# A decoder layer on eight cores: instruction order from per-stage streams and a rough clock, or from one dependency graph and a list scheduler over all engines

## The chip, the cores and the metric

The kernel runs on the 8 cores of one Trainium2 chip. Each core does the whole layer for 2 of the 16 sequences; nothing passes between cores. The metric is the device time of the slowest core, in microseconds (us).

A core has several engines that each run their own instruction list in order: PE (matrix products), DVE (vector), ACT (activation functions), POOL (a second, slower vector engine: an f32 sum of 128x512 took 1.41 us on it and 0.71 us on DVE in the profile before), SP (only starts transfers here). They wait for each other by semaphores. The order in which instructions are put in these lists is fixed when the kernel is built. A badly placed instruction stalls everything behind it in its list (in the profile before, PE once stood for 7.03 us ahead of work that did not need the wait), and this case is about that order.

The program has two states. In some executions the four cores of one die are granted a lower PE clock than the other four, and the time is longer (in the first run of the changed kernel 0.81 to 0.82 against 0.98 to 0.99 of full speed, and up to 3064 us against 2646); such a run is called slow.

## The reference

The layer is a half-weighted SwiGLU FFN, a mixer with two kinds of attention, and a second half-weighted FFN, each between two RMS norms. The sizes are 2048 tokens a sequence, width 1024, FFN width 2816.

```python
x = x + 1/2 * post1(SwiGLU_1(pre1(x)))
x = x +       post2(W_out [DiffAttn(groupA) ; DilatedAttn(groupB)])   # both from ONE projection of pre2(x)
x = x + 1/2 * post3(SwiGLU_2(pre3(x)))

def swiglu(x, w_gate, w_up, w_down):
    return (jax.nn.silu(x @ w_gate) * (x @ w_up)) @ w_down
# DiffAttn: 4 heads, causal, a = softmax(q1 k1) - lam * softmax(q2 k2), values of width 128, then a per-head RMS norm
# DilatedAttn: 8 heads of width 64, patterns (window, dilation) = (128,1), (512,4), (2048,16), mixed by their denominators
# both with ALiBi: score += -slope * distance
```

Both kernels work on 8 "units" of attention a sequence: units 0 to 3 are one differential head each (below: diff), units 4 to 7 are two dilated heads each (below: dilated). A unit is cut into steps. A step multiplies a block of keys with 512 queries on PE (these products are called scores), takes the exponential on ACT, masks or weights on DVE, and multiplies with the values on PE. A diff unit has 40 steps and a dilated one 18.

## The kernel before

Both kernels do the FFN products with 7 block products in place of 8, which needs sums and differences of weight blocks (DVE) and of activations. Half a sequence is done at a time. The order of work in the kernel before is sequence 0: FFN1, attention, FFN2; then the same for sequence 1. The sums are made for the first sequence and stored, and loaded for the second. Part of this preparation runs inside attention:

```python
def weight_sums(F, bF, SB, bS, eng, cost):          # four DVE operations a pair of weight blocks
    for j, a, b, op, rd in ((0, F(2), F(3), ALU.add, [bF[1]]), (1, SB(0), F(0), ALU.subtract, [bS[0], bF[0]]),
                            (2, F(1), SB(1), ALU.subtract, [bF[0], bS[1]]), (3, F(0), F(2), ALU.subtract, bF)):
        ...
def push_prep(s):                                   # a stream of jobs beside attention
    ...
    for j in range(len(jobs)):
        ...  # load(j + 1) on POOL's queue, the four sums on DVE, then store(j) on SP's
```

The order of instructions comes from a rough clock. `_advance` adds an assumed cost to the time of an engine, and side work waits in streams of items. An item is put in when the clock says that it would be ready within a slack:

```python
def can_run(it, force=False):
    ...
    t = S.t[PE]
    if it.eng != PE and S.t[it.eng] > t + SLACK[it.eng]:
        return False
    ...
    return S.ready(rd, wr, it.eng) <= t + SLACK[it.eng]

# main loop of attention: what does PE do next: scores, fill (projections), values
t = S.t[PE]
...
if r_s <= first + EPS_T:
    pick = "S"
elif r_f <= first + EPS_T and (fill.urgent or behind or forced or r_a > first + EPS_T):
    pick = "F"
elif r_a <= first + EPS_T:
    pick = "A"
else:
    pick = "F"
```

For the head with the steepest slope the exponential of a step is split into four, each with its own bias.

The softmax here doesn't subtract the row's maximum and nothing guards it: scores larger than these inputs give would overflow.

## Time and profile before

The first three runs took 3361.25, 3153.83 and 3228.06 us (median 3228.06). The profiled run is a fast one.

The head of the page of the profiled run: the span, the busy time of each engine, the busy tenths of PE and its granted clock in 40 equal slices, and the chain of work that ended last, by engine.

```profile
span 3091.0 us, 51661 instructions; the slowest of 8 cores (3068.5 to 3091.0 us)
...
PE 2603.4 (84%) x16608; PEld 1346.4 (44%) x16608; DVE 1671.9 (54%) x2740; ACT 1431.6 (46%) x2186; POOL 616.5 (20%) x636
...
PE   3998998667788867987999999877888887799996
...
PEclk9999999779899988998999999988899999899998
...
PE 65%; DMA 11%; DVE 10%; ACT 6%; issue 6%; SPq 1%; POOL 0%; DVEq 0%; ACTq 0%; POOLq 0%
```

PE is busy for 84%, but the chain is only 65% PE: a fifth of it is transfers and DVE. The two valleys in the row of PE (slices 8 to 15 and 27 to 34) are the two attentions, and the clock dips in the same slices. Cut by stage, as busy times in stretches (columns: stretch and length, then busy us and instruction count of PE, its weight loads, DVE, ACT and POOL, then granted clock, DMA share, GB/s): the two attentions are lines one and four; lines two and three are a gate/up half of the FFN with sums remade, and one with sums loaded.

```profile
510.40:1146.50 636.10, 470.12 (x4233) 274.89 (x4232) 354.00 (x694) 339.77 (x523) 88.55 (x133) 0.89 0.54 121
1394.50:1550.10 155.60, 141.13 (x619) 61.56 (x620) 109.41 (x143) 61.08 (x82) 61.95 (x54) 0.95 0.58 128
1830.70:1966.80 136.10, 133.77 (x619) 60.20 (x618) 79.19 (x101) 62.37 (x85) 49.92 (x38) 1.00 0.69 210
2058.90:2631.20 572.30, 460.04 (x4231) 269.93 (x4231) 310.63 (x609) 330.48 (x508) 58.21 (x92) 0.92 0.33 79
```

In attention no engine is near full: PE is busy 470 of 636 us and 460 of 572 us, so 278 us of PE idle in the two, and DVE and ACT 53 to 58%. A gate/up half that remakes its sums took about 20 us longer than one that loads them, at a clock of 0.95 against 1.00. The waits of PE in the first attention (columns: engine, line, releaser: us in all, times, longest us; in the tile names, ps is the kernel's tensor in PSUM, to which PE writes its products, and M the one in SBUF, from which PE reads its operands):

```profile
PE ps L739 <- DVE M L732: 20.9, 2, 10.5
PE ps L1569 <- DVE M L1586: 16.3, 14, 2.3
PE ps L1272 <- DVE M L1241: 15.6, 6, 10.8
PE ps L1371 <- ACT M L1393: 14.2, 16, 2.7
```

There is no single large wait. There are many releasers, and the longest waits are 7 to 11 us, far longer than the operations waited for (those in these lines take 0.4 to 1.3 us in the mean). The timeline of PE shows one (start us, busy us, operation; in brackets the idle time before and its releaser). PE stands for 7 us before four transposes, although projections, which don't need them, follow in its list:

```profile
652.29 0.63 PE L1410 MATMUL ps<-M 128*128 128x129 bf16 x8
659.95 0.58 PE L1471 MATMUL ps<-ident,M 128*128 128x128 f16 x4 [7.03 <-DVE M L1282]
```

In the FFN, PE waits for weight sums, and DVE waits until the store of older sums has read its buffer. From the waits of the whole run:

```profile
PE ps L1013 <- DVE M L887: 46.2, 14, 14.3
...
DVE M L887 <- DMA sgu<-M: 47.5, 14, 11.0
```

Two groups of DVE instructions: the post-norm multiply and the normalisation of the dilated heads (count, then busy us and mean ns, then idle time before).

```profile
L805 DVE SCALAR_TENSOR_TENSOR M<-M,gains 128x512 f16<-128x512 f16 x192 | 206.9, 1106 | 20.3 <-ACT M L746 20.2
...
L1586 DVE TENSOR_TENSOR M<-ps,M 64x512 f16<-64x512 f32 x64 | 82.9, 1295 | 123.4 <-ACT M L1582 100.7 <-PE ps L1232 13.0 <-ACT sml L1451 6.0
```

### The profile page before, as it was taken

What the parts mean: (1) busy time and instruction counts of PE and PEld (TensorE: products, weight loads), DVE (VectorE), ACT (ScalarE), POOL (GpSimd) and SP (SyncE); (2) the same over time, 40 slices, a digit from 0 to 9 for tenths busy, and PEclk for the clock granted to TensorE, in tenths of its full rate; (3) what the DMA queues carried; (4) which work ended last, traced back from release to release, by engine and by line L of the source; (5) the groups of instructions that cost most, each with busy time, mean ns of one, the idle gap of its engine ahead of it and who ended that gap; (6) DMA issues with size and microseconds to landing.
All of it is one profiled execution on the core that took longest, in us unless ns stands there. A gap on an engine that the chain in (4) does not pass through costs nothing.

```text
span 3091.0 us, 51661 instructions; the slowest of 8 cores (3068.5 to 3091.0 us)
## 1 busy us (share of the span) xinstructions
PE 2603.4 (84%) x16608; PEld 1346.4 (44%) x16608; DVE 1671.9 (54%) x2740; ACT 1431.6 (46%) x2186; POOL 616.5 (20%) x636
## 2 busy tenths in 40 slices
PE   3998998667788867987999999877888887799996
PEld 1443444334455423433444444554555553344455
DVE  4554652735455577647646456456354656644733
ACT  2443343555455553443444444435765456344442
POOL 0322411122100024304204114011011001410411
PEclk9999999779899988998999999988899999899998
DMA  5876964399713257577468667794311223656868
GB/s 113 167 162 123 198 117 82 95 214 204 182 28 57 62 151 179 140 204 173 90 191 264 173 211 224 224 262 125 83 19 32 56 56 118 211 144 202 264 178 266
DMA packets 241111, 466.95 MB, mean 151 GB/s; under 512 B 39632, under 2 KB 62416, under 8 KB 240848
## 3 DMA queue, kind: packets, MB, share of 16 engines
q1 hardware_dynamic: 203632, 362.90, 38.1%
q0 software_dynamic: 37216, 100.74, 21.0%
q8 instruction: 141, 2.31, 0.3%
q14 instruction: 122, 1.00, 0.1%
HBM read 447.10 MB, written 110.89 MB: 181 GB/s over the span
## 4 chain that ended last, share of the span: by engine, by line
PE 65%; DMA 11%; DVE 10%; ACT 6%; issue 6%; SPq 1%; POOL 0%; DVEq 0%; ACTq 0%; POOLq 0%
PE ps L1013 33%; PE ps L1081 9%; PE ps L1272 6%; PE ps L1118 4%; PE ps L1410 3%; DMA sdn<-M 3%; PE ps L1232 2%; PE ps L1308 2%; DVE M L805 2%; PE ps L1569 2%; DMA M<-xT 2%; DMA M<-sdn 2%; DMA sgu<-M 2%; PE ps L1371 2%; ACT M L1393 2%
## 5 line engine op out<-in xcount | busy, mean ns | idle before, releaser
L1013 PE MATMUL ps<-M 128*128 128x512 f16 x4928 | 1096.2, 384 | 100.7 <-DVE M L887 46.2
L1013 PEld LDWEIGHTS ps<-M 128*128 128x128 f16 x4928 | 484.1, 99 | 710.9 <-issue 151.1
L1081 PE MATMUL ps<-M 128*128 128x512 f16 (+1 forms) x2464 | 417.8, 331 | 31.8 <-DMA M<-sdn 17.8
L1393 ACT ACTIVATE M<-ps,btab 128x256 bf16<-128x256 f32 (+3 forms) x512 | 350.9, 712 | 193.8 <-PE ps L1371 165.6
L939 POOL TENSOR_TENSOR M<-M 128x512 f16<-128x512 f32 x176 | 243.3, 1384 | 661.6 <-ACT M L935 661.5
L732 DVE TENSOR_TENSOR M<-M 128x512 bf16<-128x512 bf16 x336 | 145.9, 436 | 389.3 <-ACT M L730 372.1
L824 POOL TENSOR_TENSOR M<-M 128x512 f32<-128x512 f32 x146 | 203.2, 1406 | 648.1 <-DVE M L805 304.2
L1081 PEld LDWEIGHTS ps<-M 128*128 128x128 f16 x2464 | 243.7, 100 | 203.2 <-issue 43.6
L1272 PE MATMUL ps<-M 128*128 128x512 f16 x1024 | 267.9, 402 | 50.0 <-DVE M L1241 25.4
L948 DVE TENSOR_TENSOR M<-M,ps 128x512 f16<-128x512 f32 x176 | 120.7, 686 | 346.1 <-PE ps L1013 294.7
L935 ACT ACTIVATE M<-M 128x512 f32<-128x512 f32 x176 | 110.8, 630 | 404.5 <-DVE M L956 404.4
L952 ACT ACTIVATE M<-ps 128x1024 f32<-128x1024 f32 x176 | 179.8, 1022 | 231.4 <-PE ps L1013 203.3
L887 DVE TENSOR_TENSOR M<-M 128x1024 f16<-128x1024 f16 (+1 forms) x280 | 212.6, 777 | 122.8 <-DMA sgu<-M 47.5
L956 DVE TENSOR_TENSOR M<-ps,M 128x1024 f32<-128x1024 f32 x176 | 214.2, 1221 | 68.9 <-PE ps L1013 68.7
L1537 ACT ACTIVATE M<-ps 128x1024 bf16<-128x1024 f32 x144 | 140.4, 1007 | 183.3 <-PE ps L1530 169.6
L730 ACT ACTIVATE M<-M 128x512 bf16<-128x512 f32 (+1 forms) x280 | 163.1, 622 | 128.4 <-DVE M L824 38.7
L805 DVE SCALAR_TENSOR_TENSOR M<-M,gains 128x512 f16<-128x512 f16 x192 | 206.9, 1106 | 20.3 <-ACT M L746 20.2
L1410 PE MATMUL ps<-M 128*128 128x129 bf16 x2176 | 183.9, 230 | 26.0 <-DVE M L1397 15.0
L1232 PE MATMUL ps<-M 128*128 128x128 f16 x2048 | 157.5, 233 | 22.8 <-DVE M L769 10.7
L1410 PEld LDWEIGHTS ps<-M 128*128 128x128 bf16 x2176 | 136.8, 102 | 84.2 <-issue 76.8
L862 DVE TENSOR_TENSOR M<-M 128x512 f16<-128x512 f16 (+1 forms) x328 | 162.4, 536 | 8.7 <-DVE M L862 0.7
L1272 PEld LDWEIGHTS ps<-M 128*128 128x128 f16 x1024 | 93.7, 101 | 160.3 <-issue 81.7
(72 smaller groups left out, 2383.3 us busy)
## 6 DMA issues: line engine op xcount, KB each, us to landing
M<-sdn SPq DMA_DIRECT2D x224, 352.0 KB, 4.9
M<-sgu SPq DMA_DIRECT2D x308, 256.0 KB, 3.0
M<-wgu POOLq DMA_DIRECT2D x108, 512.0 KB, 9.5
M<-x SPq DMA_DIRECT2D x96, 512.0 KB, 8.3
sgu<-M SPq DMA_DIRECT2D x66, 512.0 KB, 5.1
M<-xT SPq DMA_DIRECT2D x64, 512.0 KB, 10.8
x<-M SPq DMA_DIRECT2D x64, 512.0 KB, 5.9
sdn<-M SPq DMA_DIRECT2D x48, 352.0 KB, 7.3
```

The source lines that it names most:

```text
L805: S.op(DVE, lambda e: e.scalar_tensor_tensor(self.yb[d][0], self.yi[d][0], gains[:, self.gcol + d:self.gcol + d + 1], rst[ri], ALU.mult, A ...
L824: S.op(eng, lambda e: e.tensor_tensor(xt.ap(d), xt.ap(d), yb[d][0], ALU.add), reads=[xt.buf(d), yb[d][1]], writes=[xt.buf(d)], cost=1.4 if ...
L887: eng, lambda e: e.tensor_tensor(SB(j), a, b, op), reads=rd, writes=[bS[j]], cost=cost),
L939: S.op(POOL, lambda e: e.tensor_tensor(hs(p, l), t[:, 0:512], t[:, 512:1024], ALU.mult), reads=bt, writes=[B_H[p][l]], cost=1.3)
L952: S.op(ACT, lambda e: e.activation(o, bank(b, 2), AF.Copy), reads=[B_ps[b], B_ps[b + 1]], writes=bo, cost=c_act(1024))
L956: S.op(DVE, lambda e: e.tensor_tensor(o, bank(b, 2), o, ALU.add), reads=[B_ps[b], B_ps[b + 1]] + bo, writes=bo, cost=c_dve(1024))
L1013: S.op(PE, lambda e, g=g, kc=kc, pb=pb, src=src, piece=piece, n=n: e.matmul(bank(pb + g), src[:, g * 512 + kc * 128:g * 512 + (kc + 1) * 1 ...
L1081: S.op(PE, lambda e, k=k, pb=pb, w=w, piece=piece, n=n: e.matmul(bk(pb), w.ap[:, k * 128:(k + 1) * 128], H[piece][:, k * 512 + c0:k * 512 ...
L1232: S.op(PE, lambda e, kc=kc: e.matmul(bank(pb)[:, tq * 128:(tq + 1) * 128], xn[:, kc, t * 128:(t + 1) * 128], wap[:, kc * 128:(kc + 1) * 12 ...
L1272: S.op(PE, lambda e, kc=kc: e.matmul(bank(pb), wap[:, kc * 128:(kc + 1) * 128], xn[:, kc, ts(tt)], start=(kc == 0), stop=(kc == NKC - 1)), ...
L1393: S.op(ACT, lambda e, o_=o_, i_=i_, bias=bias: e.activation(o_, i_, AF.Exp, bias=bias, scale=SCALE), reads=rd + [B_const], writes=[bP], co ...
L1410: S.op(PE, lambda e, a_ap=a_ap, m=m, uq=uq, first=first: e.matmul(a_ap, P[:, m, uq * 128:(uq + 1) * 128], Vt[i][:, kt, 0:w1], start=(kt == ...
```

## The change

The intent is to let one scheduler order everything. All operations are first recorded as nodes of a graph, with the engines that could do each and a duration for each. The graph is then run through a simulation of all engines, and the instruction lists are written in the order of simulated start. Beside that the work is regrouped: both FFN1 (four halves), one attention stream over all 16 units with diff and dilated units alternating, both FFN2. The stored sums are dropped and the sums remade for each half; the FFN2 weights are copied to 16 bits by transfers during attention. The head with the steep slope gets one exponential a step and a multiplication by a strip of factors on DVE.

The diff rewrites most of the file. Its core, cut and reordered by subject ("..." marks cuts):

```diff
-    def ready(self, reads, writes, eng=PE):
-    def _advance(self, eng, reads, writes, cost):
-        def can_run(it, force=False): ...
-        def pump(limit=6, only=None): ...
-        def push_prep(s): ...
-        def down_plain(h, stats, after): ...
+L_TO = {PE: 0.15, ACT: 0.095, DVE: 0.105, POOL: 0.145, SP: 0.15}
+class Graph:
+    def _add(self, rd, wr, nom, tag): ...          # predecessors from the buffers read and written
+    def schedule(self):
+        ...
+        for n in reversed(nodes):                   # latest start, carried backward
+            ...
+            best = n.nom
+            for s in n.succ:
+                v = s.prio - c - lat
+                if v < best:
+                    best = v
+            n.prio = best
+        ...
+        while left:
+            ...                                     # the engine that can start something first
+            lim = m + DELTA[e]                      # among what can start within DELTA: lowest prio
+            ...
+            n.eng, n.start, n.alt = e, t, a
+            ...
+                if e == POOL:
+                    port_pool = t + c               # the model keeps POOL and the DVE operations with port set apart
+                elif e == DVE and n.port:
+                    port_dve = t + c
+            order.append(n)
+def a_ps(n):                                        # durations of ACT, DVE, POOL by size
+    return 0.171 + n * 0.000833
+def v_16(n):
+    return 0.153 + n * 0.00052
+def p_tt(n):
+    return 0.1 + n * 0.0022
...
+        ORDER = [0, 4, 1, 5, 2, 6, 3, 7]
+                    while sc_next < len(steps) and sc_next <= j + LOOK:      # LOOK = 3 scores ahead
+                        steps[sc_next][1][1]()
+                        sc_next += 1
+                    x[3]()
+                    ...
+                    while (state["f"] - f0) / fw < mdone / total[w] or (urgent and not state["open"]):
+                        if not fill_one():          # projections of the next unit, paced over this one
+                            break
...
+                    if u == 0:                      # one exponential, then the strip
+                        g.op([(ACT, a_ps(n), act_(P[:, :, c0:TT], sp[:, :, c0:TT], AF.Exp, scale=SCALE))], bs, [bP],
+                             tab="e")
+                        ...
+                        g.op([(DVE, v_16(n), tt_(P[:, :, c0:TT], P[:, :, c0:TT], t_, ALU.mult))],
+                             [bP, B_strip], [bP], port=True)
...
-        for s in range(NSEQ):
-            half_ffn(s, 0, 0)
-            half_ffn(s, 0, 1)
-            push_prep(s)
-            attention(s)
-            half_ffn(s, 1, 0)
-            half_ffn(s, 1, 1)
+        for s in range(NSEQ):
+            for h in range(2):
+                pend = ffn_half(s, 0, h, pend)
+        attention()
+        for s in range(NSEQ):
+            for h in range(2):
+                pend = ffn_half(s, 1, h, pend)
+        g.schedule()
+        g.emit()
```

## The prediction

> **What bounds the kernel now.** The profiled run lasts 3091 us; the core view grants all cores a mean clock of 0.939 to 0.944, so it is a fast run. The chain of waits is 65% PE. Cutting the timeline of PE by line gives the stages:
>
> - before the first FFN matmul: 53 us;
> - FFN, eight half-sequence passes: 1830 us;
> - attention: 636 us (first sequence), 572 us (second).
>
> Without gaps a 128x512 matmul costs 0.216 us, a 128-column one 0.056 to 0.06 us (timeline). From the instruction counts that makes about 1595 us of FFN and 740 us of attention (estimate). So FFN wastes about 235 us, attention 470 us: there the busy times by stage show PE at 74 to 80%, clock 0.89 to 0.92, ACT and DVE only 53 to 58%. No engine bounds attention; ordering does. PE's waits in it are many short ones on DVE and ACT, single ones of 7 to 11 us.
>
> FFN halves that load stored sums (second sequence) need 136 us gate/up and 70 us down at clock 1.00. Halves that remake sums need 142 to 165 us gate/up, with PE waiting for DVE (46 us, sums) and DVE for stores of sums (47 + 44 us). Two halves run down in two passes (92 and 98 us, waiting for weights).
>
> **What changes.**
> - Removed: stored sums and their preparation inside attention, plain down passes (704 matmuls become 616), one of two two-pass downs, one FFN/attention round trip, four-way split exponentials of head 0 (about -75 us of ACT).
> - Added: DVE sums everywhere, 352 of 0.68 us and 144 of about 0.89 us (estimate), +190 us; strip multiplies, +45 us; combos in all halves, +37 us. About 180 of 400 elementwise POOL operations move to DVE (0.7 us each). DVE rises from 1672 to about 2000 us. An f16 weight copy is cast during attention.
> - Moved: projections of the next unit (21 us of PE) fill every attention unit, diff and dilated alternating; scores run three steps ahead across units.
>
> **Critical path.** An FFN half holds about 180 us of DVE against 203 us of PE: tight, but the blocking stores are gone. I expect 213 us a half, 1700 us in all (-130). A diff unit has 44 us of PE against 41 us of ACT, a dilated one 33 us of PE against 31 us of DVE (estimates from durations above); with latencies 49 and 39 us, with output projections and edges 870 us (-340). Start, tail and seams: 85 us. Span about 2655 us, ratio 0.86. The clock in attention should rise: [...] the stages agree (1.00 in dense FFN, 0.89 in attention).
>
> **Time.** Runs before were 3154 to 3361 us, mixed states. I predict 2710 us, 2580 to 2880 us. Faster by over 2%: 0.94; within 2%: 0.04; slower: 0.02.
>
> **Right or wrong shows as:** attention near 870 us, ACT and DVE over 70%, clock above 0.93; FFN halves 205 to 222 us with DVE over 85%; no waits on sum stores; first FFN matmul at 45 to 55 us; DVE busy near 2000 us.
>
> **What would break it:** DVE and POOL slowing each other (post-norm multiplies took 1.11 us in the mean, 0.75 at best), so that FFN becomes DVE-bound; in-order engines with orders fixed from wrong latencies, each slip stalling PE; cast and weight loads sharing POOL's queue[...].

1700 us of FFN, 870 of attention and 85 of start, tail and seams make the 2655 us of the span.

## More of the kernel before

The normalisation of the dilated heads writes with an inner stride of four elements:

```python
for g in range(TT // G):                            # G = group_of(slope): 128, 256 or 512
    ...
    S.op(ACT, lambda e, ...: e.activation(o_, i_, AF.Exp, bias=bias, scale=SCALE), ...)
...
S.op(DVE, lambda e, m=m, lo=lo: e.tensor_tensor(
    mixT[lo, u, ts(Q)].rearrange("p (i r) -> p r i", r=4),
    bank(4 + m)[lo].rearrange("p (r i) -> p r i", r=4),
    rec[lo].rearrange("p (r i) -> p r i", r=4), ALU.mult), ...)
```

## The result

The changed kernel gives the right output. Its six runs were 2652.21 and 2656.89 us (fast) and 2780.79, 2917.40, 3065.38 and 3067.75 us (slow); the median of all is 2849.1. The ratio of fast runs is 0.8584, with a 95% interval of 0.8535 to 0.8634. Ratios in this document are from fast runs of the same rounds; they can differ by 0.1% from what the plain means of the runs quoted give.

The head of the page after:

```profile
span 2650.7 us, 49087 instructions; the slowest of 8 cores (2640.6 to 2650.7 us)
...
PE 2478.0 (93%) x16196; PEld 1272.3 (48%) x16196; DVE 1884.0 (71%) x3207; ACT 1415.4 (53%) x2027; POOL 414.0 (16%) x453
...
PE   3999899999999989999887999999999999999997
...
PEclk9999999999999999999999999999999999999998
...
PE 82%; DVE 5%; DMA 4%; issue 4%; ACT 3%; SPq 1%; DVEq 0%; POOL 0%; ACTq 0%; POOLq 0%
```

The valleys are nearly gone and the slices with a low clock too, and the chain is 82% PE. The clock records in the two traces give half speed for 11.7% of the span before (slowest core) and 3.0% after. By stage (columns as above): FFN1, attention, FFN2 with the tail, then one diff and one dilated unit inside attention.

```profile
46.70:888.00 841.30, 814.60 (x3701) 362.83 (x3702) 639.83 (x1012) 388.13 (x570) 159.94 (x196) 0.99 0.70 140
888.00:1818.90 930.90, 854.09 (x8445) 515.33 (x8445) 559.04 (x1142) 652.55 (x907) 123.82 (x153) 0.98 0.45 97
1818.90:2650.70 831.80, 806.39 (x4035) 392.28 (x4033) 667.32 (x1019) 360.85 (x529) 126.15 (x94) 0.99 0.49 155
1494.70:1550.90 56.20, 53.79 (x567) 33.27 (x566) 21.18 (x62) 45.14 (x60) 6.29 (x9) 1.00 0.34 61
1550.90:1589.10 38.20, 36.13 (x424) 23.52 (x422) 24.23 (x43) 27.40 (x38) 3.78 (x6) 1.00 0.34 56
```

| stage, us | before | after | difference |
|---|---|---|---|
| to the first FFN matmul | 53.2 | 46.7 | -6.5 |
| FFN, eight halves, with the tail | 1829.4 | 1673.1 | -156 |
| attention, both sequences | 1208.4 | 930.9 | -277.5 |
| span | 3091.0 | 2650.7 | -440 |

Attention gave nearly two thirds of the gain. Its PE idle time fell from 278 to 77 us, and its PE busy time from 930 to 854 us at a clock of 0.98 in place of 0.89 and 0.92. The largest waits of PE in attention are now these; none but the first has a long one. (In the changed kernel L605 and L608 are helpers through which most operations of DVE and ACT go, so these lines name no one operation.)

```profile
PE ps L990 <- ACT M L608: 14.6, 10, 11.8
PE ps L1081 <- ACT M L608: 9.2, 17, 1.1
PE ps L1204 <- ACT M L608: 9.1, 14, 2.5
```

The two DVE groups shown of before are cheaper by 25% and 47%. The first meets POOL less often: counted in the traces, 107 of its 192 multiplies overlapped an operation of POOL before and took 1.39 us in the mean, and 54 after, at 1.04 us; the others took 0.74 us in both. The second now writes contiguously and reads its PSUM operand with the stride.

```profile
L709 DVE SCALAR_TENSOR_TENSOR M<-M,gains 128x512 f16<-128x512 f16 x192 | 155.0, 825 | 4.0 <-ACT M L608 3.9
...
L605 DVE TENSOR_TENSOR M<-ps,M 64x512 f16<-64x512 f32 x64 | 44.0, 687 | 23.0 <-ACT M L608 17.7 <-PE ps L1081 1.6 <-ACT sml L608 0.9
```

Why is attention 931 us where PE's columns make 740 us? The timeline of PE in a steady stretch of a diff unit, every line directly after the one before:

```profile
1042.45 0.39 PE L1081 MATMUL ps<-M 64*128 64x512 bf16 x2
1042.77 0.63 PE L1112 MATMUL ps<-M 128*128 128x129 bf16 x8
1043.26 0.59 PE L990 MATMUL ps<-M 128*128 128x512 f16 x2
1043.78 0.39 PE L1081 MATMUL ps<-M 64*128 64x512 bf16 x2
1044.10 0.61 PE L990 MATMUL ps<-M 128*128 128x512 f16 x2
1044.55 0.62 PE L1112 MATMUL ps<-M 128*128 128x129 bf16 x8
1045.10 0.39 PE L1081 MATMUL ps<-M 64*128 64x512 bf16 x2
```

Read from start to start. The two score matmuls of a pair (L1081) use 64 of the 128 rows each and run at once: the second starts 3 ns after the first in the median, and the pair takes less than twice 0.216 us. 512 columns alone take 0.216 us (216 ns from start to start in the median of the gate/up products, L802), but the next group starts 0.32 us later. Two projection matmuls (L990) take 0.45 us before value matmuls and 0.52 before scores; eight value matmuls (L1112) take 0.46 to 0.49 before projections and 0.55 before scores. Over the whole trace, groups of this size without a wait behind them take the same in the median: 0.32 us for the pair, 0.55 before scores against 0.47 elsewhere for the value matmuls, 0.53 against 0.44 for the projections. So going into a 64-row group and out of it costs about 0.1 us each, without any wait being shown. There are 464 score steps (2 sequences times 4 x 40 + 4 x 18), so up to 464 x 0.2 = 93 us (an estimate). The prediction had left this out.

### The profile page after: what moved, and what is told of

It reads as the page before. It is cut to its first block, busy times and chain, and to the rows that moved or that the text cites. A ratio compares the mean times of both kernels' runs of the same rounds, so it can differ in the third digit from the quotient of the medians.

```text
span 2650.7 us, 49087 instructions; the slowest of 8 cores (2640.6 to 2650.7 us)
## 1 busy us (share of the span) xinstructions
PE 2478.0 (93%) x16196; PEld 1272.3 (48%) x16196; DVE 1884.0 (71%) x3207; ACT 1415.4 (53%) x2027; POOL 414.0 (16%) x453
## 4 chain that ended last, share of the span: by engine, by line
PE 82%; DVE 5%; DMA 4%; issue 4%; ACT 3%; SPq 1%; DVEq 0%; POOL 0%; ACTq 0%; POOLq 0%
PE ps L802 36%; PE ps L867 19%; PE ps L990 8%; PE ps L1112 5%; PE ps L963 4%; PE ps L1025 4%; DVE M L605 3%; ACT M L608 3%; PE ps L1081 3%; PE ps L1241 2%; PE ps L1204 1%; DMA M<-x 1%; SPq L156 1%; DMA lamv<-c_lam 1%; DMA M<-xT 1%
## 5 line engine op out<-in xcount | busy, mean ns | idle before, releaser
L605 DVE TENSOR_TENSOR M<-M 128x512 bf16<-128x512 bf16 (+7 forms) x1652 | 982.8, 630 | 233.9 <-ACT M L608 89.2
L802 PE MATMUL ps<-M 128*128 128x512 f16 x4928 | 1080.4, 381 | 23.4 <-DVE M L605 16.6
L608 ACT ACTIVATE M<-ps 128x512 f32<-128x512 f32 (+6 forms) x937 | 681.9, 760 | 529.9 <-PE ps L867 173.0
L802 PEld LDWEIGHTS ps<-M 128*128 128x128 f16 x4928 | 480.8, 98 | 617.4 <-issue 50.6
L608 ACT ACTIVATE M<-M 128x512 f32<-128x512 f32 (+2 forms) x640 | 387.0, 627 | 564.3 <-DVE M L605 424.7
L867 PE MATMUL ps<-M 128*128 128x512 f16 (+1 forms) x2772 | 542.6, 357 | 0.2 <-DVE M L605 0.2
L605 POOL TENSOR_TENSOR M<-M 128x512 f32<-128x512 f32 (+1 forms) x220 | 290.8, 1326 | 1161.2 <-DVE M L709 507.3
L867 PEld LDWEIGHTS ps<-M 128*128 128x128 f16 x2772 | 271.8, 98 | 264.6 <-issue 5.3
L605 DVE TENSOR_TENSOR M<-ps,M 128x1024 f32<-128x1024 f32 (+3 forms) x312 | 302.6, 972 | 127.2 <-PE ps L867 69.5
L990 PE MATMUL ps<-M 128*128 128x512 f16 x1024 | 265.0, 384 | 16.0 <-ACT M L608 14.6
L608 ACT ACTIVATE M<-ps,btab 128x1024 bf16<-128x1024 f32 x240 | 227.8, 983 | 45.5 <-PE ps L1081 41.5
L1112 PE MATMUL ps<-M 128*128 128x129 bf16 x2176 | 170.6, 224 | 10.9 <-DVE M L605 7.6
L605 DVE TENSOR_TENSOR M<-M,ps 128x512 f16<-128x512 f32 x176 | 119.7, 682 | 67.6 <-PE ps L802 49.3
L1112 PEld LDWEIGHTS ps<-M 128*128 128x128 bf16 x2176 | 132.7, 99 | 60.7 <-issue 43.4
L667 DVE SCALAR_TENSOR_TENSOR M<-M,gains 128x512 f16<-128x512 f32 x192 | 133.5, 744 | 12.3 <-ACT M L608 10.7
L990 PEld LDWEIGHTS ps<-M 128*128 128x128 f16 x1024 | 87.5, 98 | 102.4 <-issue 38.3
L963 PEld LDWEIGHTS ps<-M 128*128 128x128 f16 x2048 | 121.1, 99 | 29.5 <-issue 22.2
L608 ACT ACTIVATE ps<-ps 128x1024 f32<-128x1024 f32 (+2 forms) x110 | 100.8, 916 | 56.6 <-PE ps L867 45.2
L1025 PE MATMUL ps<-M 128*128 128x512 f16 x512 | 120.2, 385 | 5.5 <-ACT M L608 3.2
```

What stands on the lines that cost most here:

```text
L605: return lambda e: e.tensor_tensor(o, a, b, op)
L608: return lambda e: e.activation(o, i, f, **k)
L667: g.op([(DVE, v_stt(512), lambda e, o=o, kc=kc: e.scalar_tensor_tensor(o, halves(xt.ap(kc)), gains[:, gcol + kc:gcol + kc + 1], halves(rst ...
L802: g.pe([(lambda e, gg=gg, kc=kc, pb=pb, src=src, piece=piece, n=n: e.matmul(bank(pb + gg), src[:, gg * 512 + kc * 128:gg * 512 + (kc + 1) ...
L867: g.pe([(lambda e, k=k, pb=pb, src=src, piece=piece, n=n: e.matmul(bk(pb), src[:, k * 128:(k + 1) * 128], H[piece][:, k * 512 + c0:k * 512 ...
L963: g.pe([(lambda e, kc=kc: e.matmul(bank(pb)[:, tq * 128:(tq + 1) * 128], xn[:, kc, t * 128:(t + 1) * 128], wap[:, kc * 128:(kc + 1) * 128] ...
```

## The experiments

Each is an edit of the changed kernel unless said otherwise, and is correct unless said otherwise. The first eight were made on chips whose fast runs of the kernel before took 3087 to 3113 us; they are comparable with each other. The last four ran on a chip that granted every kernel, the one before too, a mean clock of only 0.87 to 0.92 in its better runs. Nearly all of their runs count as slow, since one die is mostly 1 to 4% longer than the other at a lower clock. They are read only against the kernel before on that chip, as indications, on the runs in which neither die fell still lower (below called the better runs).

In the profiled runs of rough_costs and pair_start2 on that chip the clock was lower in the FFN, where PE is denser, than in attention. On the slowest core of rough_costs it was 0.85 in FFN1 with PE busy over 99%, against 0.93 in attention with 89%; on that of pair_start2 0.89 and 0.81 in the two FFN stages with 99 and 98%, against 0.92 with 88%. In the changed kernel, on another chip, both FFN stages had 0.99 with PE busy 97%. By stage, FFN1 and attention of rough_costs:

```profile
49.20:992.40 943.20, 939.48 (x3702) 393.52 (x3703) 631.06 (x1024) 393.79 (x570) 138.67 (x182) 0.85 0.62 126
992.40:1988.80 996.40, 882.99 (x8444) 537.43 (x8444) 542.87 (x1113) 667.18 (x937) 123.00 (x156) 0.93 0.41 91
```

So there the stage with the fuller PE had the lower clock, and ratios from that chip can't be set beside those of the others.

### full_row: scores with all 128 rows (wrong result)

The two score matmuls use 128 rows and half of the columns each, so that the columns per pair stay the same and PE never changes between 64-row and 128-row matmuls. The scores are wrong (relative error 0.58).

```diff
-                        sp[:, m, c0:TT], KT[i][64 * m:64 * m + 64, kt * 128:(kt + 1) * 128],
-                        QT[i][64 * m:64 * m + 64, Q * TT + c0:(Q + 1) * TT], start=True, stop=True),
+                        sp[:, m, (c0, c1)[m]:(c1, TT)[m]], KT[i][:, kt * 128:(kt + 1) * 128],
+                        QT[i][:, Q * TT + (c0, c1)[m]:Q * TT + (c1, TT)[m]], start=True, stop=True),
 ... the same for the dilated units
```

> Wrong result on purpose: the scores use all 128 rows and half the columns, so each score step streams as many columns as before, but never switches the array between 64-row and 128-row matmuls. Theory A (my 740 us for attention left out a cost of about 0.2 us for each of the 464 score steps, about 93 us, seen as 0.32 instead of 0.216 us for a score pair and 0.56 instead of 0.46 us for what stands before it): attention falls from 927 us to 835 to 880 us, FFN stays within 10 us of 1677 us. Rival B [...]: attention stays within 15 us of 927 us.

The fast runs took 2626.5 to 2630.0 us, ratio 0.8476 (0.8441 to 0.8511). The timeline of PE in the same stretch, then attention by stage:

```profile
1043.30 0.38 PE L1082 MATMUL ps<-M 128*128 128x256 bf16 x2
1043.51 0.59 PE L990 MATMUL ps<-M 128*128 128x512 f16 x2
1043.94 0.62 PE L1113 MATMUL ps<-M 128*128 128x129 bf16 x8
1044.40 0.38 PE L1082 MATMUL ps<-M 128*128 128x256 bf16 x2
```

```profile
893.40:1791.50 898.10, 806.77 (x8444) 562.95 (x8444) 558.20 (x1140) 647.10 (x906) 123.62 (x153) 0.96 0.45 101
```

A score pair now takes 0.21 to 0.22 us and eight value matmuls before scores 0.46: the cost of the switch is there, 0.1 us each way, and it is this that went. PE's busy time in attention fell by 47 us (854 to 807), but attention by only 33 us (931 to 898). Neither stated range was met. With the switches gone the diff units at full clock take 50 to 53 us with ACT busy 81 to 85% in them (75 to 80% in the changed kernel), the clock fell from 0.98 to 0.96, and PE's idle time rose from 77 to 91 us, in waits for ACT and DVE. So the cost is real, but the part of it that was had here is about a third of the 93 us.

### no_sums: no remade sums (wrong result)

The seven products use unsummed weight blocks, so that the DVE work of the sums disappears (relative error 0.81).

```diff
-            weight_sums(lambda i: F[i], bF, lambda j: SS[j][0], [x[1] for x in SS], v_16(m))
-            return ((F[0], bF[0]), SS[0], SS[1], (F[1], bF[0]), SS[2], SS[3], (F[3], bF[1]))
+            return ((F[0], bF[0]), (F[0], bF[0]), (F[1], bF[0]), (F[1], bF[0]), (F[2], bF[1]), (F[2], bF[1]), (F[3], bF[1]))
```

> Wrong result on purpose: no weight sums are made, PE reads the plain blocks in their place; all else stays. Theory A (remaking sums is hidden under PE): the DVE share in FFN falls from about 85% to about 60%, but the FFN stages fall by less than 40 of 1677 us. Rival B (FFN is now bound by DVE): they fall by more than 60 us, towards 1595 us.

The fast runs took 2654.6 to 2657.7 us, ratio 0.8569: no change. FFN1 by stage:

```profile
57.80:873.00 815.20, 805.84 (x3702) 362.17 (x3703) 488.23 (x783) 383.97 (x568) 150.46 (x195) 1.00 0.73 144
```

DVE lost 152 us in FFN1 and 176 in FFN2. The FFN as a whole became 18 us shorter, the start 11 and attention 10 us longer. So always remaking the sums is hidden behind PE. The prediction had called the FFN "tight" on DVE; by this run it was not.

### split_exp: four exponentials again for the steep head

```diff
-                    if u == 0:
-                        g.op([(ACT, a_ps(n), act_(P[:, :, c0:TT], sp[:, :, c0:TT], AF.Exp, scale=SCALE))], bs, [bP], tab="e")
-                        ... the strip multiplication on DVE
+                        G = group_of(sl)
+                        for gr in range(TT // G):
+                            ... one activation with its own bias for each group, as in the kernel before
```

> Undoes one part: the exponentials of head 0 in four pieces with biases again, in place of one exponential and the strip multiply on DVE. About 28 us more ACT work in each of the two head-0 units. Theory A (a diff unit runs at the pace of ACT and PE together, so extra ACT shows in full): 35 to 55 us slower in attention. Rival B (idle ACT time elsewhere takes it up): under 12 us.

The fast runs took 2655.1 and 2663.1 us, ratio 0.8575. Attention by stage:

```profile
889.40:1819.40 930.00, 858.76 (x8444) 519.38 (x8444) 522.79 (x1098) 694.00 (x1093) 120.24 (x154) 0.98 0.46 98
```

ACT does 41 us more and DVE 36 us less, and attention is the same to a microsecond. My expectation failed. The strip is worth nothing in time that shows: the added work of ACT found room.

### fill_first: projections not paced

All projections of the next unit are put in as early as buffers allow instead of being spread over the unit.

```diff
-                    while (state["f"] - f0) / fw < mdone / total[w] or (urgent and not state["open"]):
+                    while fillq or (urgent and not state["open"]):
```

> Undoes one part: the projections of the next unit are put right behind the first step of a unit, not paced over it; the same work, buffers and scheduler. Theory A (the gain in attention comes from spreading projections between score and value steps, so that PE has work while ACT makes exponentials): attention grows by 100 to 250 us, PE idle and a lower clock in the second part of each unit. Rival B (the list scheduler reorders by readiness anyway, or LOOK alone suffices): under 30 us.

The fast runs took 2676.0 to 2686.4 us, ratio 0.8642 (0.8599 to 0.8685). Attention took 947.8 us (+17) and the FFN 1687.1 (+14). A pair of units took 52.1 + 47.1 us where the changed kernel takes 56.2 + 38.2. My expectation of 100 to 250 us failed. Presumably the limited fill banks and the order by readiness in the simulation spread the projections anyway; that is argued from the code, not shown.

### prio_order: the same graph, not simulated

Priorities are carried backward as in the changed kernel, and the lists are written in order of priority. Each operation takes the first engine of its alternatives. No simulated time decides anything.

```diff
+    def by_priority(self):
+        ... # succ and prio as in schedule()
+        for k, n in enumerate(nodes):
+            n.alt = n.alts[0]
+            n.eng = n.alt[0]
+        self.order = sorted(nodes, key=lambda n: (n.prio, n.i))
...
-        g.schedule()
+        g.by_priority()
         g.emit()
```

> The same graph of instructions, but the clock model of the engines is taken out: instructions are put out in the order of their latest allowed start alone (the nominal PE time carried back through the graph), and each takes its first engine choice. Theory A (simulating all engines with measured durations is what closes the gaps): over 60 us slower, with PE waiting on single instructions that stand too early in another engine's order. Rival B (the structure of the program, nominal times, lookahead and buffers, does it, the simulation only refines): within 40 us of 2651 us.

The fast runs took 3182.8 and 3184.6 us, against 3087.1 to 3103.1 us of the kernel before in the same rounds (ratio worked out from these, 1.029). FFN1 and attention by stage, then the waits of PE in the whole run:

```profile
46.10:1015.70 969.60, 841.71 (x3712) 362.04 (x3713) 631.97 (x932) 413.85 (x606) 254.33 (x262) 0.96 0.61 121
1015.70:2197.30 1181.60, 910.52 (x8432) 520.49 (x8430) 641.14 (x1246) 570.63 (x745) 169.23 (x193) 0.91 0.32 74
```

```profile
PE ps L818 <- DVE M L621: 123.7, 45, 12.9
PE ps L883 <- DVE M L621: 57.7, 46, 5.2
...
PE ps L1175 <- DVE M L964: 32.9, 25, 3.8
```

The whole gain is gone, and more. Attention has 271 us of PE idle (1181.6 less 910.5), as much as the kernel before (278), and the clock of the kernel before (0.91). All the other parts of the change are still there: the merged attention, the alternation, the paced projections, three scores ahead, remade sums. So the regrouping by itself does not bring the gain: in this order, without simulated time, it is lost. Another order without a simulation, such as that of the old streams, was not tried on the new graph.

### one_engine: simulated order, one engine for each operation

This separates the two things that the simulation decides.

```diff
-        n.alts = [(e, c, [(fn, rd, wr, True)]) for e, c, fn in alts]
+        n.alts = [(e, c, [(fn, rd, wr, True)]) for e, c, fn in alts[:1]]
```

> The scheduler may no longer choose between engines: every operation takes its first alternative, so silu products and residual sums go to POOL again, evacuations to DVE in attention and ACT in FFN. Since dropping the weight sums gave no time at all, DVE has room: I expect under 20 us slower. The rival, that balancing work over DVE, POOL and ACT is a main source of the gain, expects over 50 us.

The fast runs took 2749.2 to 2759.4 us, ratio 0.8903 (0.8857 to 0.895). Attention took 930.8 us (the same), the FFN 1767.6 us (+94). The post-norm group, and PE's waits for weight sums and other DVE results in the gate/up products:

```profile
L709 DVE SCALAR_TENSOR_TENSOR M<-M,gains 128x512 f16<-128x512 f16 x192 | 192.5, 1032 | 6.6 <-ACT M L608 6.6
```

```profile
PE ps L802 <- DVE M L605: 53.6, 26, 5.1
```

The same wait in the changed kernel:

```profile
PE ps L802 <- DVE M L605: 16.6, 13, 3.3
```

Expected were under 20 us; it was 97. With fixed engines, POOL's busy time in the FFN is 499 us instead of 286. The same post-norm multiply takes 1.03 us instead of 0.83, the sums take 0.87 instead of 0.79 us, and PE's wait for DVE in gate/up is 53.6 us instead of 16.6. The multiply is slow where it meets POOL: in this trace 90 of the 192 overlapped an operation of POOL and took 1.36 us in the mean, where the other 102 took 0.74 us, as they do in the changed kernel. By what means is not shown. What the order alone is worth follows from the two runs on one chip: the spans of prio_order and of one_engine are 3181.3 and 2747.7 us, so 434 us at the same engines, 251 of it in attention. (With the choice of engine, the changed kernel is 531 us below prio_order.)

### two_sets and same_kind: does alternating help?

The changed kernel has one set of Q, K and V buffers for each kind of unit, so two units of a kind can't follow each other with overlap. two_sets gives both sets room for either kind (one exponential buffer fewer, 5 instead of 6) and keeps the alternation: a control. same_kind uses that room for the old order, diff first.

```diff
-NPB = 6
+NPB = 5
-                i = 0 if isd else 1
+                i = ORDER.index(u) % 2
 ... buffers moved to make the room
 ... same_kind also:
-        ORDER = [0, 4, 1, 5, 2, 6, 3, 7]
+        ORDER = [0, 1, 2, 3, 4, 5, 6, 7]
```

A first build of same_kind had a race: DVE wrote an output tile that an earlier operation of DVE reads, without waiting for that read. In both kernels, and in prio_same and pair_start2, an engine now also waits for its own reads of these tiles.

> Control for the next kernel: the attention buffers for queries, keys and values are two general sets used in turn (ones written again for each unit, five probability buffers instead of six, a second gathered-value buffer), with the units still alternating in kind. Expected within 15 us of the changed kernel, 2651 us.

> As the control, but the units of a sequence run in the order of before: four differential ones, then four dilated ones. Theory A (alternation only saves buffers; every unit window holds the same kind of main work and 21 us of projections either way): within 15 us of the control. Rival B (alternation balances ACT-heavy and DVE-heavy units): over 30 us slower than the control.

two_sets took 2656.9 to 2672.6 us (ratio 0.8605, attention 927.7), same_kind 2644.9 to 2684.4 us (ratio 0.8588, 0.8496 to 0.8681, attention 923.7). Alternating the kinds saves buffers. It saves no time that shows; the interval of same_kind is about 1% either way.

### prio_same, rough_costs and before_no_prep, on the chip with the low clock

These three ask what remains: whether the simulation's choice of engine is enough when the order is by priority (prio_same), how exact the durations must be (rough_costs: 1.3 us for any POOL operation, 0.7 us for any other elementwise one), and what the preparation of sums cost in the attention of the kernel before (before_no_prep, an edit of the kernel before, wrong, relative error 0.67).

```diff
 prio_same:
+    def by_priority(self):
+        self.order = sorted(self.nodes, key=lambda n: (n.prio, n.i))
         g.schedule()
+        g.by_priority()
 rough_costs:
-        n.alts = [(e, c, [(fn, rd, wr, True)]) for e, c, fn in alts]
+        n.alts = [(e, 1.3 if e == POOL else 0.7, [(fn, rd, wr, True)]) for e, c, fn in alts]
 before_no_prep (against the kernel before; the loads that would read stored sums read other data of that size):
+            done_tags.add(("prep", s))
+            return
             for j in range(len(jobs)):
```

> Separates the two things that the priority-order kernel took away: here the simulation still chooses the engine of every operation (the same choices as in the changed kernel), but the order in which instructions are put out is again by latest allowed start alone. Theory A (the order from simulated time is the main part): 3050 to 3250 us. Rival B (the engine choice is the main part): below 2850 us.

> The scheduler stays, but its measured durations are replaced for every ACT, DVE and POOL operation by a constant (0.7 us, on POOL 1.3 us); PE and DMA costs stay. Theory A (it takes measured durations, since the engines run in order and every slip reaches PE): 60 to 250 us slower than 2651 us, mostly in FFN, where DVE is busiest. Rival B (a list schedule of roughly right costs suffices): under 40 us slower.

> Wrong result on purpose: the kernel before, with the preparation of stored weight sums inside attention taken out; the passes that load these sums load other stored sums of the same size. It tells how much of the lost time in attention came from the preparation, not from the order. My prediction listed it as removed work in attention. Expected: attention of the first sequence from 636 to 570 to 590 us, of the second from 572 to 550 to 565 us, 60 to 90 us together of the 277 us that the change gained there.

The kernel before took 3289.4 to 3294.5 us there in its better runs. prio_same took 3271.5 to 3295.4 us in its better runs, the same as the kernel before, and die by die it is within 1% too: the choice of engine in an order by priority brings no gain over the kernel before, as with prio_order (the two can't be compared across clocks). rough_costs took 2943.6 to 2973.6 us, about 0.90 of the kernel before (0.89 and 0.90 on the two dies), where the changed kernel has 0.858 on the other chips. That is not the worth of exact durations: pair_start2 below, which has them, has 0.887 on the same chip, and the changed kernel was not timed there. So most of the gain survives rough durations, and what exact ones add stays open. before_no_prep took 3199.1 to 3210.0 us, 2.6% or about 85 us less than the kernel before. Its trace puts the two attentions at 574.9 and 545.0 us, where the profile of the kernel before has 636.1 and 572.3 on another chip: 88 us less, the first as expected and the second a little more. That indicates that preparation was a part of the old attention's cost, and about a third of the 277 us gained there.

### pair_start2: two score steps together, and an earlier start

Two score steps are put together, so that PE changes between 64-row and 128-row matmuls half as often (0.1 us each way in the changed kernel), and the transfers at the start wait in the order in which they are needed.

```diff
-                        steps[sc_next][1][1]()
-                        sc_next += 1
+                        pair = [st_[1][1]() for st_ in steps[sc_next:sc_next + 2]]
+                        g.pe([o for b in pair for o in b["pe"][0]], sum(b["pe"][1] for b in pair) + 0.2)
+                        for b in pair:
+                            b["cont"]()
+                        sc_next += 2
...
-                    g.dma(POOL, [(v, src)], [], [b], m)
+                    g.dma(POOL, [(v, src)], [[B_XR[6]], [B_XR[10]], []][(k > 1) + (k > 4)], [b], m)
```

> The refused try at a better kernel, mended: where an output tile is written by the engine that last read it, that engine now waits for its own read. Two changes: (1) the scores of two steps are issued as one block, so the array switches between 64-row and 128-row matmuls half as often (about 0.2 us for each of 232 pairs, 46 us of PE); (2) constants and the weights of later blocks are not loaded before the first input tiles. Expected: attention 15 to 35 us below 931 us, first FFN matmul at 38 to 43 us in place of 47 us, FFN within 10 us of 1673 us. Rival: a pair has to wait for both score banks, so ACT starves and attention is no faster, or up to 20 us slower.

It ran on the chip with the low clock too: 2911.1 to 2930.2 us, against 3279.9 to 3291.6 us of the kernel before in its better runs (about 0.887). One diff unit in a stretch where the clock was full:

```profile
1573.70:1633.20 59.50, 53.67 (x567) 32.96 (x566) 23.08 (x64) 42.81 (x55) 7.42 (x11) 1.00 0.34 64
```

A pair of steps put together takes 0.54 us from start to start instead of twice 0.32, as intended. Yet at a full clock a diff unit takes 58.5 to 60.1 us, against 54.5 to 56.2 in the changed kernel, and PE is busy in it for 53.7 to 53.9 us, no less than there (52.2 to 54.3). The likely reason is that a pair has to wait until both score buffers are free; that was the rival's expectation, and no run isolates it. The first FFN matmul came at 41.3 us instead of 46.7. Whether the start alone would give a faster kernel was not tried, and no version here is shown to beat the changed kernel with correct results.

## Why the prediction was right or wrong

**The time.** It said 2710 us (2580 to 2880), faster. The fast runs are 2652 and 2657 us, the median of all six, mixed states, is 2849. The span was put at about 2655 us and was 2650.7. The extra 2% seems to come from taking the 3154 us run for a fast one (0.86 of it is 2712); it was slow, and a fast run is only 1.5 to 2 us longer than the span of its slowest core.

**What bounds the kernel: right, and shown for the new graph.** "No engine bounds attention; ordering does." Writing the same graph in another order costs 434 us at the same choice of engines (one_engine to prio_order), and in attention it brings back as much PE idle time and as low a clock as in the kernel before. That this is near the whole gain of 440 us is chance, since prio_order is slower than the kernel before. For the kernel before itself the reading rests on its profile: no engine full, many waits; its own order was not exchanged alone.

**Attention at 870 us: wrong, 931.** The step that failed is the estimate of "about 740 us" of attention without gaps, and with it "a diff unit has 44 us of PE". It counted columns and left out the change between 64-row and 128-row matmuls, 0.1 us each way and up to 93 us in all (an estimate, from 464 score steps). A diff unit at full clock took 54.5 to 56.2 us instead of the predicted 49, a dilated one 36 to 38 instead of 39. Taking the change away (full_row) gave back 33 of the 61 us missing. By these units about 36 of the 61 us lie in the 16 units (an estimate: 8 pairs of some 92.5 us in place of 88); the rest, in output projections and edges, has no shown cause.

**FFN at 1700 us plus 85 us for start, tail and seams: too much.** Both together were 46.7 + 1673.1 = 1720 us, 65 less than the 1785 predicted. This cancels the 61 us missing in attention, so the good total rests partly on two errors of opposite sign. The halves took 202 to 220 us, five of the eight inside the range stated (205 to 222) and three just below it.

**DVE at about 2000 us and over 85% in the FFN: wrong.** It was 1884 us, and 76% and 80% in the two FFN stages. Two terms make up 91 of the 116 us: the post-norm multiplies became 0.825 us (-52 us), mostly because the choice of engine keeps them apart from POOL (54 of 192 met it, against 90 and 1.03 us in one_engine), and the normalisation became 0.687 us (-39 us) with its new access pattern. The fear that FFN would be bound by DVE was unfounded: no_sums takes away 328 us of DVE work there and the FFN gains 18.

**The means named for the gain: mostly not the means.** Pacing the projections is worth about 25 us (fill_first), the single exponentials nothing that shows (split_exp), the alternation nothing that shows (same_kind), remade sums cost nothing that shows (no_sums), and the old preparation accounts for about 85 us if the chip with the low clock is representative. Each of these looked like a cause in the diff.

**The choice of engine: undervalued.** It is worth 97 us, all of it in the FFN, against an expected 20 or less.

**Signs that held.** Waits for stores of sums are gone; the first FFN matmul came at 46.7 us; ACT is busy 70% of attention (DVE 60%, not over 70); the clock in attention is 0.98. For the last, the prediction had the stages before: 1.00 in dense FFN, 0.89 in attention. In the attentions on the first chips a busier PE went with a higher clock: 0.89 and 0.92 with PE busy 74 and 80% before, 0.98 with 92% after, and 0.91 again in prio_order with 77%. On the chip with the low clock it did not: there the FFN1 of rough_costs had 0.85 with PE busy over 99%, and its attention 0.93 with 89%. What sets the clock is not shown.

**What stays open.** The exact worth of accurate durations; how much of the old attention's 278 us of idle PE was its own order, since the orders tested without simulated time were by priority and not those of the old streams; the separate worth of the 16-bit weight copy and of merging the two attentions, which no run undid; whether the order alone would help the kernel before without the regrouping; and whether the earlier start gives a faster kernel.

## What to carry to other kernels

When PE, ACT and DVE are all well under full and the waits are many, short and of many kinds, the instruction order is what to work on: record everything as a graph, simulate all engines with durations from the trace (how exact they must be is open), and write the lists in simulated order. Let the simulation choose between DVE, ACT and POOL, with a model that keeps DVE and POOL apart (the post-norm multiply took 0.74 us away from POOL and 1.04 to 1.39 us beside it). When PE time is estimated from columns, add the changes between 64-row and 128-row matmuls (0.1 us each way here), and test each attractive part of a change by undoing it alone, because here most of them were worth nothing that shows.
